# Fetching the norm factors of a hybrid decoder step as rows through DRAM instead of broadcasting them with matrix products

## The chip, the cores and the metric

The kernel runs on one core of a Trainium2 chip. The core has a matrix engine (TensorE, PE in the profile, with its weight loads as PEld), a vector engine (VectorE, DVE), a scalar engine (ScalarE, ACT), a general engine (GpSimd, POOL) and SyncE (SP), which here only issues DMA transfers, in order, and waits before each for what the transfer needs. ScalarE issues a few transfers as well. The metric is the device time of one launch in microseconds, as the median of several runs; lower is better.

## The reference

One layer of a hybrid decoder, run on 2048 prompt tokens and on 8 single tokens of a decode batch, all in fp32. What matters for this change are its five RMS norms:

```python
def _rmsnorm(x, g):
    xf = x.astype(jnp.float32)
    y = xf * lax.rsqrt(jnp.mean(xf * xf, axis=-1, keepdims=True) + EPS) * g.astype(jnp.float32)
    return y.astype(x.dtype)
...
    xn = _rmsnorm(x, norm1_g)
    z = jnp.einsum('btd,de->bte', xn, w_in)
    xr, gr, q, k, v = jnp.split(z, IN_SPLITS, axis=-1)
...
    rec = (hs * jax.nn.gelu(gr.astype(jnp.float32))).astype(x.dtype)
...
    mix = jnp.concatenate([_rmsnorm(rec, rec_norm_g), _rmsnorm(att, attn_norm_g)], axis=-1)
    h = x + jnp.einsum('bte,ed->btd', mix, w_out)
    hn = _rmsnorm(h, norm2_g)
    ff = jax.nn.silu(jnp.einsum('btd,df->btf', hn, w_gate)) * jnp.einsum('btd,df->btf', hn, w_up)
    y = h + jnp.einsum('btf,fd->btd', ff, w_down)
...
    y_prompt = _rmsnorm(yp, final_norm_g)
    y_sample = _rmsnorm(ys, final_norm_g)
```

`hs` is a gated linear recurrence over the tokens behind a short convolution, `att` a sliding-window attention with sinks. The model width is 1024, the two groups are 512 wide each, and the FFN is 2816 wide.

## The kernel before

**Layout and precision.** Activations lie transposed: features on the 128 partitions, tokens along the free dimension. A norm factor is one number per token, so it must be had on all 128 partitions as a row along the tokens before VectorE can multiply with it. The large products run in a fast fp32 mode on operands split into a high and a low part, three products for each pair; the small ones run in plain fp32, where the profile shows each as two instructions.

**First stage, the mixer.** The 2056 tokens are cut into four sub-blocks (`SUBS`: 520, 512, 512, 512 tokens). For each sub-block s the input projection runs as 14 units of 128 output columns (`unit`, L746, products named ip), in the order of `ORDERS[s]`: units 0 to 3 feed the recurrence, 4 to 7 the gate branch, 8 and 9 k and v, 10 to 13 q. A unit accumulates in one of three PSUM banks (pool `ps_acc`) and VectorE evacuates it with a multiplication by the row of factors of the first norm (L763). A gate unit is evacuated into `rrec`, of which there is one buffer for all sub-blocks, so the gate units of sub-block s wait until the group norm of sub-block s - 1 has scaled the old contents (the key `("rc", s - 1)`). Recurrence, attention, group norms (`group_norm`, L847), the output projection (`out_unit`, L1071; `out_half` for the last sub-block; products op) and the sum of squares for the second norm follow.

**Second stage, the FFN.** The tokens are cut again, into three blocks of two halves (`HALVES`: twice 344, then four times 342). `hn_mix` (L507) reads the residual stream `hs` back from DRAM, scales it with the factors of the second norm (L521), forms the sums and differences of a seven-product scheme (Strassen's) and stores them in DRAM as `mixed`; `hn_load` brings them back and splits them. For each block, 11 pairs of FFN chunks run gate, up (ps_g, ps_u) and down products (pd, pw), with y accumulated in SBUF by VectorE (L1469, L1500). `finish` (L1502) ends the first two blocks: it adds up squares, makes the final norm's factors, scales y (L1520) and stores it. `y_load` (L1214) then brings the residual stream of the next block into the same buffers. The third block ends in `finish_last`.

**How a factor row is made.** `rstd_cols` (L445) multiplies the accumulated squares with a column of averages on TensorE, which leaves one factor per partition in a few columns (104 x 5, 128 x 4, 86 x 4 or 114 x 3), adds epsilon on VectorE and raises to the power -0.5 on GpSimd (L454). For the first norm of sub-blocks 1 to 3 the squares come from ScalarE's accumulation instead (`norm_rows`, L656). Then `row_bcast` (L456) makes the row: for each column one plain fp32 product of the column, broadcast over 128 output rows, with the identity matrix, into the only bank of `ps_m`; ScalarE copies the result to SBUF (L470), into one of three buffers of `bcp`. `half_bcast` (L479) does the same for a half of a block of the second stage, from the factors `rs2` of all sub-blocks that it touches (copy at L494, two buffers of `hbp`).

**What sets the order of the work.** Every chain of work is a generator with planned times; the planned time becomes the priority with which a scheduler orders each engine's instructions. TensorE's order through the mixer and the start of the FFN is written out by hand in `PE_ORDER` (name and count of each product, from L112), with the broadcast products bc_x2, bc_x3, bc_rc1, bc_rc2 and the second norm's hb_0_0 and hb_0_1 in their places; later TensorE work is ordered by the scheduler. SP's transfers are ordered by the scheduler too, and a waiting transfer holds up all behind it.

Of the kernel before, what the change touches and what calls it, by code (L numbers as in the profile page):

```python
# [7 lines left out]
F32 = mybir.dt.float32  # L8
# [5 lines left out]
P = 128  # L14
# [4 lines left out]
NTOK = SEQ + NB  # L19
# [127 lines left out]
op0_6_260:2 s7_1_0:3 op0_6_260:10 op0_7_0:24 op0_7_260:3 o6_1_0 bc_x2_0:3 pt6_1_1 o6_1_0 bc_x2_0 op0_7_260 pt6_1_1:3  # L147
op0_7_260:11 o6_1_1 op0_7_260:9 ip2_4_0:24 o6_1_1 ip2_0_0:5 pt7_0_0:4 ip2_0_0:10 st_h0:5 ip2_0_0:2 o7_0_0 ip2_0_0:4
o7_0_0 ip2_0_0:3 ip2_5_0:4 pt7_0_1 st_rc1:2 pt7_0_1:3 st_rc1:2 ip2_5_0:9 pt7_1_0:4 ip2_5_0:2 o7_0_1 ip2_5_0:3 o7_0_1
bc_rc1_0:4 ip2_5_0:3 o7_1_0 ip2_5_0:3 pt7_1_1:3 ip2_1_0:2 pt7_1_1 ip2_1_0:8 g2_0_0_0 ip2_1_0:8 o7_1_0 ip2_1_0:4  # L150
# [7 lines left out]
op1_4_0:20 op1_5_0:3 pt9_0_1:4 op1_5_0 o9_0_0:2 op1_5_0:16 o9_0_1 op1_5_0:4 op1_6_0:2 bc_x3_0:2 s10_1_0 bc_x3_0:2  # L158
# [3 lines left out]
op1_7_0:8 s11_0_0 pt10_0_0:2 o9_1_1 s11_0_1 st_rc2:4 s11_0_1 op1_7_0:2 s11_0_1:2 op1_7_0:7 bc_rc2_0:4 op1_7_0:6  # L162
ip3_12_0 o10_0_0 ip3_12_0:3 o10_0_0 pt10_0_1:4 ip3_12_0:12 o10_0_1 ip3_12_0:3 s11_1_0:3 ip3_12_0:5 ip3_10_0:8
s11_1_1:4 pt10_1_0 st_h1:4 pt10_1_0:3 s11_1_0 ip3_10_0:4 o10_0_1 ip3_10_0:3 hb_0_0:4 ip3_10_0:6 o10_1_0 ip3_10_0:3
ip3_9_0 pt10_1_1 o10_1_0 pt10_1_1:3 ip3_9_0:8 hb_0_1:4 ip3_9_0:6 o10_1_1 ip3_9_0:9 ip3_11_0:2 o10_1_1 ip3_11_0
# [122 lines left out]
def hybrid_step(tc, xT, xR, vecs, cst, gatew, win, wout, wgate, wup, wdown, kT, vC, ck, cv, sconv, sh0,  # L288
# [4 lines left out]
    with ExitStack() as ctx:  # L293
# [54 lines left out]
        mixed = dp.tile([3, 7, P, 4, TP], F32, name="mixed")  # L348
        split_s = {x: dp.tile([NPAIR, 4, P, 2, 512], F32, name=f"split_{x}") for x in "gu"}
# [128 lines left out]

        def half_bcast(gi, n, name):  # L479
            o, nn = HALVES[gi][n]  # L480
            out = hbp.tile([P, TP], F32, tag="hb", name=f"hb_{name}")
            ps = m_tile(f"hb_{name}")
            for s, (c0, T, _, w, nt) in enumerate(SUBS):
                a, b = max(o, c0), min(o + nn, c0 + T)
                if a >= b:
                    continue
                j0, j1 = (a - c0) // w, (b - c0 - 1) // w + 1
                with ahead():
                    for j in range(j0, j1):
                        x, y = max(a, c0 + j * w), min(b, c0 + j * w + w)  # L490
                        d0 = x - c0 - j * w
# [93 lines left out]
        with ExitStack() as actx:  # L585
# [70 lines left out]
            def norm_rows(s, acc, sums):  # L656
                _, T, _, w, nt = SUBS[s]
                cols = ap1.tile([P, 5], F32, tag="xcols", name=f"xcols{s}")
                if s:
                    nc.vector.scalar_tensor_tensor(cols[:, :nt], sums[:, 0], EPS, sums[:, 1], ALU.add, ALU.add)  # L660
                    nc.gpsimd.tensor_tensor(cols[:, :nt], cols[:, :nt], nhalf[:, :nt], op=ALU.pow)
# [185 lines left out]
            def group_norm(s, raw, gcol, k0, name, t, keys, late=False):  # L847
                _, T, _, w, nt = SUBS[s]
                acc = None
                for c in range(CR):  # L850
                    yield (t - 8 + 2 * c,) + keys(c)
                    if c == 0:
                        acc = accp.tile([P, TM], F32, tag="acc", name=f"{name}acc{s}")
                    add_square(acc, raw[:, c, :T], T, c == 0, f"{name}{s}_{c}", nc.vector if s in V_GN else None)
                yield t
                cols = ap1.tile([P, 5], F32, tag=f"{name}cols", name=f"{name}cols{s}")
                rstd_cols(acc[:, :T], w, nt, 1, cols[:w, :nt], f"{name}{s}")
                bc = row_bcast(cols[:w, :nt], w, nt, f"{name}{s}")
                if late:
                    state[s]["late"] = bc  # L860
                    fire((name, s, "bc"))
                    return
                for c in range(CR):
                    yield t + 3 + c
                    v = raw[:, c, :T]
                    nc.vector.scalar_tensor_tensor(v, v, col(gcol + c), bc[:, :T], ALU.mult, ALU.mult)
# [204 lines left out]
            def out_unit(s, m):  # L1071
# [106 lines left out]
        with ExitStack() as bctx:  # L1178
# [323 lines left out]
            def finish(gi, n, t, dt):  # L1502
# [12 lines left out]
                yield t + dt * (F_FIN[2] + F_FIN[3])  # L1515
                bc = row_bcast(cols[:w, :nt], w, nt, name, 0, False, True)
# [65 lines left out]
            def last_norm(s):  # L1582
# [13 lines left out]
                rstd_cols(acc[:, :T], w, nt, 0, rs2[:w, s, :nt], f"h{s}", 0, True)  # L1596
                fire(("h", s))
# [132 lines left out]
```

## Time and profile before

| what | value |
|---|---|
| median of 3 runs | 2063.03 us (2059.93 to 2065.46) |
| span of the profiled execution | 2054.6 us |
| time of the profiled execution itself | not given; only its span is |
| TensorE busy | 2015.9 us, 98% |
| VectorE busy | 1459.9 us, 71% |
| ScalarE, GpSimd busy | 944.6 us (46%), 906.5 us (44%) |
| mean granted TensorE clock | 0.997 |
| DMA | 450.98 MB, mean 219 GB/s |

The span runs from the first to the last instruction of the profiled execution; the median, from other executions, is 8.4 us longer. All times inside the kernel count from the start of the span. Roughly, the mixer lasts until 690 us, with an overlap into the FFN, and the three FFN blocks end near 1150, 1610 and 2054 us. In a tile's row the numbers after the count are the shortest, median and longest duration in ns and the first and last start in us; in a row of the timeline or the chain they are start and duration in us. Matmuls are pipelined, so their durations overlap, and the chain shows what each adds. "Landing" is the time from the issue of a transfer until its data has arrived.

### The profile page before, as it was taken

How to read it: one execution, taken by the hardware profiler on the slowest of the kernel's cores; microseconds unless marked ns; L12 is line 12 of the kernel's file. 1: busy time of each engine (PE TensorE's matmuls, PEld its weight loads, DVE VectorE, ACT ScalarE, POOL GpSimd, SP SyncE). 2: the span in 40 equal slices, each digit the busy share in tenths (PEclk: the TensorE clock that was granted, in tenths of full speed). 3: DMA queues.
4: the chain of work that ended last, by engine and by line, in shares of the span. 5: the costliest groups of instructions: out<-in, count | busy, mean ns of one | idle time of the engine just before them, and what ended most of it. 6: DMA issues, size and time to landing. Idle time of an engine off the chain costs nothing.

```text
span 2054.6 us, 34857 instructions
## 1 busy us (share of the span) xinstructions
PE 2015.9 (98%) x12319; PEld 1908.1 (93%) x12319; DVE 1459.9 (71%) x2694; ACT 944.6 (46%) x1960; POOL 906.5 (44%) x799
## 2 busy tenths in 40 slices
PE   9999999999999999999999999999999999999998
PEld 9988787878777899999999999999999999999998
DVE  6877886767985766666654667777768666777675
ACT  6764774553664543343334533333335433433343
POOL 5311342020122787567656645556457522322333
PEclk9999999999999999999999999999999999999999
DMA  9864584576688856666546677776677675566652
GB/s 329 293 213 143 188 275 159 175 233 210 208 261 280 314 200 223 205 210 207 207 172 210 229 260 258 227 229 221 222 253 265 211 251 189 183 197 196 197 179 96
DMA packets 208991, 450.98 MB, mean 219 GB/s; under 512 B 25232, under 2 KB 82720, under 8 KB 208800
## 3 DMA queue, kind: packets, MB, share of 16 engines
q1 hardware_dynamic: 205184, 445.73, 65.2%
q10 hardware_dynamic: 3632, 3.02, 0.4%
q8 instruction: 97, 1.59, 0.3%
q14 instruction: 78, 0.64, 0.1%
HBM read 335.89 MB, written 113.84 MB: 219 GB/s over the span
## 4 chain that ended last, share of the span: by engine, by line
PE 77%; DVE 9%; DMA 6%; ACT 3%; issue 2%; POOL 1%; SPq 0%; DVEq 0%; ACTq 0%; POOLq 0%
PE ps_u L396 19%; PE ps_g L396 19%; PE pw L396 11%; PE pd L396 10%; PE ip L396 10%; PE op L396 4%; DMA n<-hs 3%; DMA xs<-in_xT 1%; DMA m<-mixed 1%; PE o L396 1%; PE pt L401 1%; DVE sc L974 1%; DVE sc L963 1%; PE s L396 1%; DMA mixed<-n 1%
## 5 line engine op out<-in xcount | busy, mean ns | idle before, releaser
L396 PE MATMUL ps_g<-hn,w_g 128*128 128x342 f32 (+1 forms) x2772 | 489.4, 320 | 4.6 <-DVE c_u L1410 1.8
L396 PE MATMUL ps_u<-hn,w_u 128*128 128x342 f32 (+1 forms) x2772 | 479.9, 319 | 1.9 <-ACT c_u L1436 1.3
L396 PEld LDWEIGHTS ps_g<-hn,w_g 128*128 128x128 f32 x2772 | 445.1, 188 | 6.0 <-DVE c_u L1410 2.3
L396 PEld LDWEIGHTS ps_u<-hn,w_u 128*128 128x128 f32 x2772 | 444.2, 188 | 2.6 <-ACT c_u L1436 1.6
L396 PE MATMUL ip<-xn,w_in 128*128 128x512 f32 (+1 forms) x1680 | 353.4, 358 | 1.9 <-ACT xn L431 1.8
L396 PEld LDWEIGHTS ip<-xn,w_in 128*128 128x128 f32 x1680 | 270.1, 189 | 46.0 <-issue 3.8
L1500 DVE TENSOR_TENSOR y<-y,pw 128x342 f32<-128x342 f32 x504 | 238.7, 504 | 73.0 <-PE pw L396 72.2
L396 PE MATMUL pd<-fh,w_d 128*128 128x344 f32 (+1 forms) x960 | 239.4, 320 | 0.6 <-DVE y L1469 0.6
L396 PE MATMUL op<-mix,w_out 128*128 128x512 f32 (+1 forms) x960 | 203.4, 357 | 0.5 <-DVE rrec L763 0.3
L396 PEld LDWEIGHTS op<-mix,w_out 128*128 128x128 f32 x960 | 155.4, 188 | 29.3 <-issue 5.0
L1469 DVE TENSOR_TENSOR y<-y,pd 128x344 f32<-128x344 f32 (+1 forms) x240 | 117.9, 507 | 75.3 <-PE pd L396 70.7
L396 PEld LDWEIGHTS pd<-fh,w_d 128*128 128x128 f32 x960 | 168.3, 188 | 1.4 <-DVE y L1469 1.1
L396 PE MATMUL pw<-fh,wd 128*128 128x342 f32 x576 | 165.6, 319 | 1.2 <-DVE y L1500 1.2
L396 PE MATMUL pd<-fl,w_d 128*128 128x344 f32 (+1 forms) x480 | 153.4, 320 | 0.0
L1381 DVE TENSOR_TENSOR fl<-c_u,fh 128x342 fp32r<-128x342 f32 (+1 forms) x132 | 107.1, 815 | 48.3 <-ACT fh L1380 47.9
L1225 POOL TENSOR_TENSOR w_u<-ru,w_u 128x512 fp32r<-128x512 f32 x44 | 58.9, 1338 | 181.6 <-ACT w_u L1224 155.0
L1392 POOL TENSOR_TENSOR c_u<-c_u,c_g 128x342 f32<-128x342 f32 (+1 forms) x60 | 60.5, 1008 | 170.7 <-DVE c_u L1410 132.1
L1380 ACT CAST fh<-c_u 128x342 fp32r<-128x342 f32 (+1 forms) x132 | 63.0, 480 | 157.8 <-POOL c_u L1392 61.9
L396 PE MATMUL pw<-t,wd 128*128 128x342 f32 x648 | 126.7, 320 | 2.6 <-DVE t L1381 1.7
L1410 DVE TENSOR_TENSOR c_u<-c_u,ps_u 128x342 f32<-128x342 f32 (+1 forms) x99 | 50.2, 507 | 100.3 <-PE ps_u L396 100.1
L396 PEld LDWEIGHTS pw<-t,wd 128*128 128x128 f32 x648 | 106.0, 188 | 4.4 <-DVE t L1381 2.5
L396 PEld LDWEIGHTS pw<-fh,wd 128*128 128x128 f32 x576 | 105.3, 189 | 1.7 <-DVE y L1500 1.5
(316 smaller groups left out, 3507.4 us busy)
## 6 DMA issues: line engine op xcount, KB each, us to landing
w_g<-split_g SPq DMA_DIRECT2D x88, 512.0 KB, 4.2
w_u<-split_u SPq DMA_DIRECT2D x88, 512.0 KB, 4.9
w_in<-split_w SPq DMA_DIRECT2D x84, 512.0 KB, 3.5
rg<-in_wgate SPq DMA_DIRECT2D x110, 256.0 KB, 3.1
ru<-in_wup SPq DMA_DIRECT2D x110, 256.0 KB, 3.2
w_out<-split_w SPq DMA_DIRECT2D x48, 512.0 KB, 4.4
split_g<-w_g SPq DMA_DIRECT2D x44, 512.0 KB, 3.6
split_u<-w_u SPq DMA_DIRECT2D x44, 512.0 KB, 2.7
```

What stands on the lines that cost most here:

```text
L396: r = nc.tensor.matmul(*args, **kw)
L401: r = nc.tensor.transpose(*args)
L963: seen[f"sm{gb}_{kv}_{g}"] = nc.vector.tensor_tensor_reduce(sc[:, g, :kn], ps[:, gi * 256:gi * 256 + kn], mask[:, k0:k0 + kn], -SCALE, ns[ ...
L974: nc.vector.tensor_scalar(sc[:, g, :kn], sc[:, g, :kn], mx[:, 1, g:g + 1], None, ALU.mult)
L1225: lo_eng.tensor_tensor(w[:, 1, :], src, w[:, 0, :].bitcast(F32), op=ALU.subtract)
L1380: nc.scalar.copy(hi, v)
L1381: nc.vector.tensor_tensor(lo, v, hi.bitcast(F32), ALU.subtract)
L1392: (nc.vector if p == NPAIR - 1 or src is not v else eng(E_MUL[2 * h + n])).tensor_tensor(v, src, g, op=ALU.mult)
L1410: nc.vector.tensor_tensor(o, a, b, op)
L1469: r = nc.vector.tensor_tensor(ys[gi, n, m], ys[gi, n, m], ps, ALU.add)
L1500: nc.vector.tensor_tensor(v, v, ps, ALU.add)
```

## The change

Some rows of factors no longer come from broadcast products. Their columns are stored to DRAM as a row of single words, and a second transfer reads the row back onto all 128 partitions. Both transfers are issued by SP. This holds for the first norm of sub-blocks 2 and 3 (x2, x3), the recurrent group's norm of sub-blocks 1 and 2 (rc1, rc2), all six half rows of the second norm, and the final norm of the first two blocks. The second norm's factors are stored once for each of the four sub-blocks, as soon as they are made. The other rows keep the broadcast products. In `finish` the planned delay ahead of the row goes as well.

```diff
+        rows_h = dp.tile([1, NTOK], F32, name="rows_h")
...
+        def rows_out(row, cols, w, nt):
+            nc.sync.dma_start(row.rearrange("o (j p) -> p (o j)", p=w), cols)
+
+        def dram_bcast(cols, w, nt, name):
+            row = dp.tile([1, w * nt], F32, name=f"row_{name}")
+            rows_out(row, cols, w, nt)
+            out = bcp.tile([P, TM], F32, tag="bc", name=f"rb_{name}")
+            nc.sync.dma_start(out[:, :w * nt], row.to_broadcast([P, w * nt]))
+            return out
+
+        def h_rows(s):
+            c0, T, _, w, nt = SUBS[s]
+            rows_out(rows_h[:, c0:c0 + T], rs2[:w, s, :nt], w, nt)
+
         def half_bcast(gi, n, name):
             o, nn = HALVES[gi][n]
             out = hbp.tile([P, TP], F32, tag="hb", name=f"hb_{name}")
-            ps = m_tile(f"hb_{name}")
-            for s, (c0, T, _, w, nt) in enumerate(SUBS):
...
-                        mm(f"hb_{name}", ps[:, x - o:y - o], rs2[:w, s, j:j + 1].to_broadcast([w, P]),
-                                         ident[:w, d0:d0 + y - x], start=True, stop=True)
-            nc.scalar.copy(out[:, :nn], ps[:, :nn])
+            nc.sync.dma_start(out[:, :nn], rows_h[:, o:o + nn].to_broadcast([P, nn]))
             return out
...
-                state[s]["bc"] = row_bcast(cols[:w, :nt], w, nt, f"x{s}")
+                state[s]["bc"] = (dram_bcast if s > 1 else row_bcast)(cols[:w, :nt], w, nt, f"x{s}")
...
-                bc = row_bcast(cols[:w, :nt], w, nt, f"{name}{s}")
+                bc = (dram_bcast if name == "rc" and s in (1, 2) else row_bcast)(cols[:w, :nt], w, nt, f"{name}{s}")
...
                     rstd_cols(acc[:, :T], w, nt, 0, rs2[:w, s, :nt], f"h{s}")
+                    h_rows(s)
                     fire(("h", s))
...
                 rstd_cols(acc[:, :nn], w, nt, 0, cols[:w, :nt], name, 0, True)
-                yield t + dt * (F_FIN[2] + F_FIN[3])
-                bc = row_bcast(cols[:w, :nt], w, nt, name, 0, False, True)
+                bc = dram_bcast(cols[:w, :nt], w, nt, name)
...
                 rstd_cols(acc[:, :T], w, nt, 0, rs2[:w, s, :nt], f"h{s}", 0, True)
+                h_rows(s)
                 fire(("h", s))
```

In `PE_ORDER` the entries bc_x2_0, bc_x3_0, bc_rc1_0, bc_rc2_0, hb_0_0 and hb_0_1 are taken out; the rest of the order stands.

More of the change, by code (lines that the diff above doesn't have):

```diff
@@ L157 @@
 pt8_1_1:4 op1_3_0:18 op1_4_0 g2_3_1_0 op1_4_0:3 o8_1_1 s10_0_0:4 o8_1_1 s10_0_1 pt9_0_0:2 s10_0_1:3 pt9_0_0:2
-op1_4_0:20 op1_5_0:3 pt9_0_1:4 op1_5_0 o9_0_0:2 op1_5_0:16 o9_0_1 op1_5_0:4 op1_6_0:2 bc_x3_0:2 s10_1_0 bc_x3_0:2
+op1_4_0:20 op1_5_0:3 pt9_0_1:4 op1_5_0 o9_0_0:2 op1_5_0:16 o9_0_1 op1_5_0:4 op1_6_0:2 s10_1_0
 s10_1_0:3 op1_6_0:2 o9_0_1 op1_6_0 s10_1_1:4 op1_6_0 pt9_1_0:2 op1_6_0:3 pt9_1_0:2 op1_6_0:5 ip3_8_0 op1_6_0 ip3_8_0
@@ L161 @@
 op1_6_0 o9_1_0 op1_6_0 ip3_8_0 pt9_1_1 o9_1_0 ip3_8_0:5 pt9_1_1:3 ip3_8_0:9 op1_7_0 o9_1_1 s11_0_0:3 pt10_0_0:2
-op1_7_0:8 s11_0_0 pt10_0_0:2 o9_1_1 s11_0_1 st_rc2:4 s11_0_1 op1_7_0:2 s11_0_1:2 op1_7_0:7 bc_rc2_0:4 op1_7_0:6
+op1_7_0:8 s11_0_0 pt10_0_0:2 o9_1_1 s11_0_1 st_rc2:4 s11_0_1 op1_7_0:2 s11_0_1:2 op1_7_0:7 op1_7_0:6
 ip3_12_0 o10_0_0 ip3_12_0:3 o10_0_0 pt10_0_1:4 ip3_12_0:12 o10_0_1 ip3_12_0:3 s11_1_0:3 ip3_12_0:5 ip3_10_0:8
-s11_1_1:4 pt10_1_0 st_h1:4 pt10_1_0:3 s11_1_0 ip3_10_0:4 o10_0_1 ip3_10_0:3 hb_0_0:4 ip3_10_0:6 o10_1_0 ip3_10_0:3
-ip3_9_0 pt10_1_1 o10_1_0 pt10_1_1:3 ip3_9_0:8 hb_0_1:4 ip3_9_0:6 o10_1_1 ip3_9_0:9 ip3_11_0:2 o10_1_1 ip3_11_0
+s11_1_1:4 pt10_1_0 st_h1:4 pt10_1_0:3 s11_1_0 ip3_10_0:4 o10_0_1 ip3_10_0:3 ip3_10_0:6 o10_1_0 ip3_10_0:3
+ip3_9_0 pt10_1_1 o10_1_0 pt10_1_1:3 ip3_9_0:8 ip3_9_0:6 o10_1_1 ip3_9_0:9 ip3_11_0:2 o10_1_1 ip3_11_0
 pt11_0_0:4 ip3_11_0:16 vt3_0 ip3_11_0:5 ip3_13_0:3 pt11_0_1 o11_0_0:2 ip3_13_0 pt11_0_1:3 ip3_13_0:4 vt3_1
@@ L481, in half_bcast @@
             out = hbp.tile([P, TP], F32, tag="hb", name=f"hb_{name}")
-            ps = m_tile(f"hb_{name}")
-            for s, (c0, T, _, w, nt) in enumerate(SUBS):
[L484 to L491, printed above, removed]
-                        mm(f"hb_{name}", ps[:, x - o:y - o], rs2[:w, s, j:j + 1].to_broadcast([w, P]),
-                                         ident[:w, d0:d0 + y - x], start=True, stop=True)
-            nc.scalar.copy(out[:, :nn], ps[:, :nn])
+            nc.sync.dma_start(out[:, :nn], rows_h[:, o:o + nn].to_broadcast([P, nn]))
             return out
```

4 lines of the change are left out of this document (2 added, 2 removed).

## The prediction

> **What bounds the kernel now.** I read the page first, engines and chain.
>
> ```profile
> PE 2015.9 (98%) x12319; PEld 1908.1 (93%) x12319; DVE 1459.9 (71%) x2694; ACT 944.6 (46%) x1960; POOL 906.5 (44%) x799
> PE 77%; DVE 9%; DMA 6%; ACT 3%; issue 2%; POOL 1%; SPq 0%; DVEq 0%; ACTq 0%; POOLq 0%
> ```
>
> TensorE is busy for 98% of the span, and 77% of the chain that ended last is TensorE's own work. Busy alone proves little, since matmul ends are modelled, but the chain agrees: an instruction taken out of TensorE's stream is worth its pitch wherever TensorE is what ends last. The stages (columns: PE, PEld, DVE, ACT, POOL, clock, DMA share, GB/s) show where it isn't.
>
> ```profile
> 600.00:650.00 50.00, 47.13 (x233) 37.66 (x232) 37.94 (x78) 28.52 (x60) 16.45 (x14) 1.00 0.83 269
> 650.00:700.00 50.00, 45.65 (x244) 39.78 (x243) 36.89 (x50) 21.45 (x44) 27.84 (x20) 1.00 0.96 344
> ```
>
> At the passage from the mixer to the FFN the DMA engines are at 0.83 to 0.96 and TensorE stands idle for 2.87 + 4.35 = 7.2 us. A matmul removed there only lengthens the idle time.
>
> **What goes.** The tiles that the change takes from TensorE, the first two in windows that hold sub-blocks 2, 3 and 1, 2 alone, the last in one that holds the first two block ends alone:
>
> ```profile
> L396 PE MATMUL bc_x<-cs,xcols x16: 270/275/275, 294.5 to 438.8; 128*128 128x128 f32 x16
> L396 PE MATMUL bc_rc<-cs,rccols x16: 270/275/275, 318.4 to 459.8; 128*128 128x128 f32 x16
> L396 PE MATMUL hb<-cs,rs x44: 166/275/356, 473.9 to 1158.1; 128*128 128x128 f32 x16, 104*128 104x104 f32 x8, 104*128 104x32 f32 x2, 104*128 104x72 f32 x2
> L396 PE MATMUL bc_f<-cs,cols_f x28: 239/275/275, 1183.7 to 1639.3; 86*128 86x86 f32 x16, 114*128 114x114 f32 x12
> ```
>
> That is 16 + 16 + 44 + 28 = 104 instructions (each fp32 product shows as two). Their 275 ns overlap, so I take what they add to the chain:
>
> ```profile
> 459.19 0.89 PE bc_rc L396 x8
> 474.11 0.81 PE hb L396 x8
> 480.08 0.82 PE hb L396 x8
> ...
> 1153.11 0.82 PE hb L396 x8
> 1157.70 0.67 PE hb L396 x6
> ...
> 1183.85 0.86 PE bc_f L396 x8
> 1188.38 0.86 PE bc_f L396 x8
> ...
> 1634.56 0.66 PE bc_f L396 x6
> 1638.87 0.66 PE bc_f L396 x6
> ```
>
> Four rows of x2, x3, rc1, rc2 at 0.89 each are 3.56; block 0's two half rows 1.63; block 2's 1.49; the block ends 1.72 and 1.32. Block 1's 14 instructions lie off the chain; at 0.82/8 they are 1.44. Together 11.16 us. The 14 ScalarE copies go as well; ScalarE is 46% busy and I give them nothing.
>
> **What comes.** Each factor row now takes two transfers in sequence on SP: a store of 344 to 520 single words, which waits for POOL's power and scatters column by column, and a load that puts the row on 128 partitions, which waits for the store to land. (The second norm has four stores for six loads.) The trace has neither. Nearest:
>
> ```profile
> n<-hs SPq DMA_DIRECT2D x32, 171.0 KB, 3.7
> xs<-in_xT SPq DMA_DIRECT2D x24, 256.0 KB, 4.6
> out_sh_o<-q ACTq DMA_DIRECT2D x4, 4.0 KB, 2.1
> out_sconv_o<-in_sconv SPq DMA_DIRECT2D x1, 32.0 KB, 8.6
> out_phs<-carry ACTq DMA_DIRECT2D x1, 2.0 KB, 5.2
> ```
>
> The load has the size and partitions of n or xs: 3.7 to 4.6 us. The store, of 1.3 to 2 KB, lies between 2.1 (4 KB of short runs on a quiet queue) and 8.6 (short runs behind two large copies); out_phs, the nearest in size, took 5.2 at a moment of full queues. I take 3.0, nearer the quiet end, as most stores fall outside the crowded passage. With two issue gaps of about 0.2 the trip is 3.0 + 4.2 + 0.4 = 7.6 us after the power; bounds 2.1 + 3.7 + 0.4 = 6.2 and 8.6 + 4.6 + 0.4 = 13.6. Where the products stood late in TensorE's order a row can also arrive sooner than before (the second norm, below).
>
> The Trainium skill, page "DMA: Bandwidth & Descriptors", section "Anatomy of one DMA — SWDGE (gpsimd) path", gives each transfer a fixed 2.0 us and 436 GB/s: 4.6 us for the pair, an estimate. No row here is as short, and by it the sum below would be 0.8 better, since rc1 would not stall.
>
> Now user by user.
>
> *x2, x3:* hidden. The powers end long before the row is used:
>
> ```profile
> 123.76 1.02 POOL L661 TENSOR_TENSOR xcols<-xcols,nhalf 128x4 f32<-128x4 f32 x1 [7.86 <-DVE xcols L660]
> ...
> 426.13 1.02 POOL L661 TENSOR_TENSOR xcols<-xcols,nhalf 128x4 f32<-128x4 f32 x1 [5.09 <-DVE xcols L660]
> 442.79 0.57 ACT L470 COPY rb_x<-bc_x 128x512 f32<-128x512 f32 x1
> ```
>
> x3's power is done at 427.15 and the row stood ready at 443.36. Even 13.6 us leaves 2.6; without that cover the first evacuation of sub-block 3 would slip by what is missing. The load for x2 has to wait for a free row buffer (three exist), but its product stood at 294.5 and its power ends at 124.78.
>
> *rc2:* hidden. Its users are the mix tiles of the output projection of sub-block 2 and gate unit 4 of sub-block 3, eighth in ORDERS[3], seven units after the row. Unhidden it would cost what rc1 can.
>
> *rc1:* tight. Gate unit 4 is first in ORDERS[2]; its product can't be evacuated into rrec until rc1 has scaled the old contents, and it holds one of three accumulator banks until then.
>
> ```profile
> 314.71 1.01 POOL L454 TENSOR_TENSOR rccols<-rccols,nhalf 128x4 f32<-128x4 f32 x1
> 320.10 2.74 DVE L866 SCALAR_TENSOR_TENSOR rrec<-rrec,vec,rb_rc 128x512 f32<-128x512 f32 x4 [0.21 <-ACT rb_rc L470]
> 325.16 0.68 DVE L763 TENSOR_TENSOR rrec<-ip,rb_x 128x512 f32<-128x512 f32 x1
> 328.99 10.31 PE L396 MATMUL ip<-xn,w_in 128*128 128x512 f32 x42
> ```
>
> Power to scaling takes 320.10 - 315.72 = 4.4 us; the bank is free at 325.84, and the written order has 24 products of unit 8 and 18 of unit 12 (the 42) start at 328.99: 3.15 us of slack, less the 0.89 that TensorE now gains between them, 2.3. The trip adds 7.6 - 4.4 = 3.2 (bounds 1.8 and 9.2): a stall of 0.9, from nothing to 6.9. VectorE runs four scalings and three subtractions before that evacuation and may close part of it, so I charge 0.8. Behind a waiting scaling on VectorE stand the evacuations of the attention (L985, L997), for which TensorE's transposes and value products wait.
>
> *Second norm:* block 0's half rows.
>
> ```profile
> 472.02 1.02 POOL L454 TENSOR_TENSOR rs<-rs,nhalf 128x4 f32<-128x4 f32 x1 [5.47 <-DVE rs L453]
> 482.08 1.06 DVE L521 SCALAR_TENSOR_TENSOR n<-n,vec,hb 128x344 f32<-128x344 f32 x2
> ```
>
> The first mix begins 9.0 us after the power, because the hand-written order put the second half row late. The trip of 7.6 fits, with one more load. Blocks 1 and 2 find their rows in DRAM well ahead; block 1's two loads (342 KB) fall into the passage at 344 GB/s: +1.0. Their saving of 1.44 falls there too and isn't counted.
>
> *Block ends:* the power, then the scaling of y, its store, the load of the next y, the adds that free TensorE's banks.
>
> ```profile
> 1182.46 1.01 POOL L454 TENSOR_TENSOR cols_f<-cols_f,nhalf 86x4 f32<-86x4 f32 x1
> 1191.87 3.98 DVE L1520 SCALAR_TENSOR_TENSOR y<-y,vec,rb_f 128x344 f32<-128x344 f32 x8
> 1203.19 0.93 DVE L1469 TENSOR_TENSOR y<-y,pd 128x342 f32<-128x342 f32 x2 [1.90 <-DMA y<-hs]
> 1632.04 0.86 POOL L454 TENSOR_TENSOR cols_f<-cols_f,nhalf 114x3 f32<-114x3 f32 x1
> 1641.07 3.97 DVE L1520 SCALAR_TENSOR_TENSOR y<-y,vec,rb_f 128x342 f32<-128x342 f32 x8
> ```
>
> From the later power to its scaling there are 1191.87 - 1183.47 = 8.4 us at the first end and 8.2 at the second. The trip of 7.6 fits by under a microsecond. At the first end the adds already wait for y, so TensorE, 1.72 earlier, meets the same y: I count half of that saving away, 0.86.
>
> *SP's queue:* each store holds SP until its power, each load until its store has landed.
>
> ```profile
> SPq L380 <- PE ip L396: 160.1, 62, 5.2
> ```
>
> Weight loads stand behind. SP itself already waits for free buffers, 160.1/62 = 2.6 us each time and up to 5.2, and five weight buffers of 12 products cover such a wait; I charge nothing, and if the cover is gone each held load costs TensorE the excess over it.
>
> **Sum:** -11.16 + 1.44 + 0.86 + 0.8 + 1.0 = -7.1 us. The profiled span of 2054.6 becomes 2047.5. The median of the runs, 2063.03, stands 8.4 above the span (no time of the profiled run itself is given), so 2063.03 - 7.1 = 2055.9; I say 2056.
>
> **Rivals.** (a) *The saving is taken up elsewhere.* Of the 11.16, 5.2 us lie before the passage (3.56 + 1.63). If the passage is fixed by VectorE and DMA work that doesn't move with TensorE, they turn into idle time there; what is left, 1.49 + 1.32 + 0.86 - 1.0 = 2.7, gives about 2060. For it speaks the idle time of 7.2; against it that the chain before 500 us is TensorE's, so that VectorE's inputs come earlier as well.
>
> (b) *Slower: the block ends become the bound.* One mechanism: the store of a last row comes late, the scaling after it, the next y after that, and the adds leave TensorE without banks. It decides once the trip exceeds 8.4 us. With a store of 5.2, a load of 4.6, 0.4 of gaps and one SP wait of 5.2 in front it is 15.4: 7.0 and 7.2 late, 14.2 in both. An idle TensorE is also slowed afterwards:
>
> ```profile
> 204.00:212.00 8.00, 5.29 (x23) 3.19 (x23) 7.48 (x16) 6.38 (x15) 0.00 (x0) 0.93 0.00 0
> 212.00:220.00 8.00, 8.00 (x43) 7.10 (x43) 7.60 (x12) 4.18 (x8) 3.29 (x2) 0.86 0.01 2
> ```
>
> After 2.7 us of idleness the granted clock fell, which costs 8 x 0.07 + 8 x 0.14 = 1.7; twice 3.4. In all -7.1 + 14.2 + 3.4 = +10.5: 2073.5; with the upper bound of the trip behind the same wait (18.8, 21.0 late in both) 2080, and down to 2069 where one end alone is hit hard. For it speaks that by the code SP issues 16 stores and 16 loads of y there; against it that the median landings are short.
>
> The Trainium skill, same page, section "Why a DMA increments its semaphore by 16 and not by 1", says a transfer spreads over the largest number up to 16 that divides its outer size: a store of 86 columns would use 2 engines and of 114 columns 6. No row here shows such a shape; by that rule (b) would be likelier at the first end than at the second.
>
> (c) *More than the sum.* The first mix can start 9.0 - 7.6 = 1.4 to 9.0 - 6.2 = 2.8 us sooner, and its chain of loads and stores with it, so that VectorE is freer before the passage. With no charge at all (11.16 - 1.44 = 9.7) that makes 11.1 to 12.5, 2050.5 to 2052. Against it, most of that chain waits for its own loads.
>
> (d) *The store or load isn't made as said, and the products stay:* the diff removes them from the written order, which pops each by name, so this has no chance worth a share.
>
> **How the numbers follow.** About 0.3%, 6.2 us, is what a measurement of this kernel can tell from no change: faster means below 2056.8. Forecast 0.55, from 2052 to 2060; its middle lies just past the bound, and since each of the charges (0.8, 0.86, 1.0) can be nought I put 0.36 of it to faster and 0.19 to same. (a) 0.19, same. (b) 0.17, slower. (c) 0.09, faster. Faster 0.45, same 0.38, slower 0.17. The range from 2050 to 2070 leaves out most of (b), 0.15, and little else; it is the forecast's own range with (c) below and the mild end of (b) above. The forecast alone, 2052 to 2060, would hold with (a) 0.74.
>
> **What would show it.** TensorE with 104 instructions fewer; new rows on SP with landings of 2 to 5 us for the stores and about 4 for the loads; VectorE's scaling by rc1 about 8 us after the power and TensorE's unit 8 starting within a microsecond of bank release; no gap at TensorE near the two block ends. Wrong: gaps there of several microseconds, a clock below 1.00 in those stages, or idle time in the passage grown by 5 us (rival a).

## The result, and the profile after

| kernel | median | range |
|---|---|---|
| before | 2061.48 us | 2058.70 to 2065.46 (4 runs) |
| changed | 2138.47 us | 2136.63 to 2141.61 (4 runs) |

The ratio is 1.0376 (95% interval 1.0362 to 1.0391): 77 us slower, where 7 us faster was forecast. The profiled span grew from 2054.6 to 2139.8 us. (The changed kernel's lines after the new functions are numbered one to four higher.) First the page of the changed kernel, engines and chain:

```profile
PE 2030.2 (95%) x12215; PEld 1912.0 (89%) x12215; DVE 1456.5 (68%) x2694; ACT 938.3 (44%) x1946; POOL 907.2 (42%) x799
PE 61%; DMA 15%; DVE 12%; issue 4%; ACT 4%; POOL 3%; SPq 1%; DVEq 0%; POOLq 0%; ACTq 0%
```

The 104 instructions are gone (12319 to 12215), yet TensorE is busy for 14.3 us longer, and its idle time (span less busy) went from 38.7 to 109.6 us, by 70.9: together the 85.2 of the span. The chain that ended last gives DMA 15% in place of 6%.

The transfers that the change added, from the list of DMA issues (count, size, median us from issue to landing):

```profile
rows_h<-rs SPq DMA_DIRECT2D x3, 2.0 KB, 9.5
row_x<-xcols SPq DMA_DIRECT2D x2, 2.0 KB, 9.7
rb_x<-row_x SPq DMA_DIRECT2D x2, 256.0 KB, 5.5
rb_f<-row_f SPq DMA_DIRECT2D x2, 171.0 KB, 4.2
```

The loads of 171 to 256 KB take 4.2 to 5.5 us, where about 4 was forecast. The stores of 2 KB take twice as long as the loads, where 3.0 was forecast. A row's trip is seen in the timeline; here rc1, first POOL, then SP, then VectorE, then TensorE:

```profile
315.91 1.01 POOL L455 TENSOR_TENSOR rccols<-rccols,nhalf 128x4 f32<-128x4 f32 x1
```

```profile
312.41 0.33 SPq L481 DMA_DIRECT2D rows_h<-rs  x1
...
319.24 0.32 SPq L497 DMA_DIRECT2D hb<-rows_h  x1
319.66 0.38 SPq L481 DMA_DIRECT2D row_rc<-rccols  x1
...
331.11 0.32 SPq L487 DMA_DIRECT2D rb_rc<-row_rc  x1
```

```profile
320.39 0.68 DVE L1000 TENSOR_TENSOR ratt<-o,ratt 64x512 f32<-64x512 f32 x1 [0.86 <-ACT ratt L999]
336.75 2.74 DVE L869 SCALAR_TENSOR_TENSOR rrec<-rrec,vec,rb_rc 128x512 f32<-128x512 f32 x4 [15.68 <-DMA rb_rc<-row_rc]
```

```profile
339.48 0.79 PE L397 MATMUL o<-pth,vt 128*128 128x512 f32 x1 [10.54 <-ACT pth L987]
```

The power ends at 316.92. SP is then still in front of a load of the second norm that waits for its own store (312.41 to 319.24, 6.8 us), and issues rc1's store only at 319.66. The load, which waits for that store to land, goes out at 331.11: 11.4 us. It lands at 336.7. From the power to the scaling it takes 19.8 us, against 4.4 before. VectorE, which works in order, stands in front of that scaling for 15.68 us; the attention's evacuations queue behind it, and TensorE stops for 10.54 us. The mean clock granted is lower in such a stop and after it (the number ahead of the DMA share and GB/s):

```profile
328.00:336.00 8.00, 0.94 (x5) 0.42 (x3) 0.00 (x0) 0.00 (x0) 0.00 (x0) 0.83 0.53 41
336.00:344.00 8.00, 4.30 (x8) 2.37 (x9) 7.25 (x12) 5.73 (x10) 0.00 (x0) 0.53 0.51 192
```

Over the whole execution the mean granted clock is 0.981, against 0.997 before. That is enough to make TensorE busy for longer with less work: an estimate from 2015.9 us less the 11.16 saved, times 0.997/0.981, is 2037 us, and 2030.2 was measured. VectorE waits in the same way for both rows of rc, for all four rows of the block ends and once for the second norm, but not for x2 and x3 (total us, times, longest):

```profile
DVE y L1523 <- DMA rb_f<-row_f: 33.7, 4, 10.5
DVE rrec L869 <- DMA rb_rc<-row_rc: 28.7, 2, 15.7
DVE n L524 <- DMA hb<-rows_h: 7.4, 1, 7.4
```

These are 69.8 us; before, VectorE waited 3.2 us in all for the copies of such rows. At the first block end SP and VectorE read:

```profile
1231.51 0.25 SPq L481 DMA_DIRECT2D row_f<-cols_f  x1
...
1239.59 0.32 SPq L487 DMA_DIRECT2D rb_f<-row_f  x1
...
1241.96 0.26 SPq L481 DMA_DIRECT2D row_f<-cols_f  x1
...
1249.48 0.32 SPq L487 DMA_DIRECT2D rb_f<-row_f  x1
```

```profile
1243.58 4.46 DVE L1523 SCALAR_TENSOR_TENSOR y<-y,vec,rb_f 128x344 f32<-128x344 f32 x8 [10.46 <-DMA rb_f<-row_f]
...
1253.89 3.01 DVE L1523 SCALAR_TENSOR_TENSOR y<-y,vec,rb_f 128x344 f32<-128x344 f32 x6 [5.43 <-DMA rb_f<-row_f]
```

Stores of 8.1 and 7.5 us, and the second held on SP behind the first row's load until 1241.96. TensorE's two waits there are for VectorE's adds:

```profile
1248.51 0.65 PE L397 MATMUL pd<-fh,w_d 128*128 128x342 f32 x1 [4.97 <-DVE y L1473]
...
1257.38 3.79 PE L397 MATMUL ps_g<-hn,w_g 128*128 128x342 f32 x12 [4.61 <-DVE c_g L1414]
```

At the second end the two stores take 6.6 and 10.9 us, and TensorE waits 3.20 and 8.97.

### The profile page after: what moved, and what is told of

Its sections match the earlier page's. It is cut to its first block, busy times and chain, and to the rows that moved or that the text cites. A ratio compares the mean times of both kernels' runs of the same rounds, so it can differ in the third digit from the quotient of the medians.

```text
span 2139.8 us, 34674 instructions
## 1 busy us (share of the span) xinstructions
PE 2030.2 (95%) x12215; PEld 1912.0 (89%) x12215; DVE 1456.5 (68%) x2694; ACT 938.3 (44%) x1946; POOL 907.2 (42%) x799
## 4 chain that ended last, share of the span: by engine, by line
PE 61%; DMA 15%; DVE 12%; issue 4%; ACT 4%; POOL 3%; SPq 1%; DVEq 0%; POOLq 0%; ACTq 0%
PE ps_u L397 17%; PE ps_g L397 16%; PE pw L397 9%; PE pd L397 9%; PE ip L397 6%; DMA n<-hs 3%; DMA row_f<-cols_f 2%; PE op L397 1%; DMA hs<-xres 1%; DMA row_rc<-rccols 1%; DMA m<-mixed 1%; DMA mixed<-n 1%; DVE sc L977 1%; DMA rows_h<-rs 1%; DVE xn L433 1%
## 5 line engine op out<-in xcount | busy, mean ns | idle before, releaser
L397 PE MATMUL ps_g<-hn,w_g 128*128 128x342 f32 (+1 forms) x2772 | 494.2, 322 | 20.1 <-DVE c_g L1414 13.6
L397 PE MATMUL ip<-xn,w_in 128*128 128x512 f32 (+1 forms) x1680 | 358.1, 361 | 2.4 <-ACT xn L432 1.7
L397 PEld LDWEIGHTS ip<-xn,w_in 128*128 128x128 f32 x1680 | 274.4, 192 | 48.1 <-issue 4.1
L397 PE MATMUL pd<-fh,w_d 128*128 128x344 f32 (+1 forms) x960 | 241.6, 323 | 14.2 <-DVE y L1473 14.2
L1385 DVE TENSOR_TENSOR fl<-c_u,fh 128x342 fp32r<-128x342 f32 (+1 forms) x132 | 109.6, 836 | 49.1 <-ACT fh L1384 48.9
```

Of the source, the lines that this page charges most:

```text
L397: r = nc.tensor.matmul(*args, **kw)
L1385: nc.vector.tensor_tensor(lo, v, hi.bitcast(F32), ALU.subtract)
```

## The experiments

The theory after this result: the store of single words is the slow thing, and it also holds the other transfers. Rivals: any trip through DRAM is this slow, or SP's order is the cost. Each ratio is to the kernel before, run beside it, with the 95% interval.

| label | what | median us | ratio |
|---|---|---|---|
| e1_runs16 | as changed, stores as 16-byte runs | 2071.91 | 1.0055 (1.0034 to 1.0076) |
| e2_dead_stores | before, plus the word stores, unread | 2095.71 | 1.0171 (1.0145 to 1.0198) |
| e7_dead_runs16 | the same as 16-byte runs | 2059.43 | 1.0003 (0.9992 to 1.0014) |
| e11_dead_apart16 | e2, words 16 bytes apart | 2058.58 | 1.0000 (0.9987 to 1.0013) |
| e10_dead_apart64 | e2, words 64 bytes apart | 2059.07 | 0.9995 (0.9985 to 1.0005) |
| e8_dead_apart | e2, words 512 bytes apart | 2058.27 | 1.0001 (0.9990 to 1.0012) |
| e4_x_h_only | as changed, x2, x3, second norm only | 2083.40 | 1.0115 (1.0097 to 1.0134) |
| e3_act_queue | as changed, rows issued by ScalarE | 2127.27 | 1.0330 (1.0309 to 1.0350) |
| e12_rc2_later | as changed, rc2 scaling planned later | 2123.96 | 1.0314 (1.0292 to 1.0335) |
| e13_same | the changed kernel again | 2128.06 | 1.0327 (1.0311 to 1.0342) |
| e14_rc2_held | as changed, rc2 scaling moved | 2119.93 | 1.0289 (1.0274 to 1.0305) |
| e15_act_again | e3 again, beside e13 | 2127.69 | 1.0317 (1.0299 to 1.0335) |
| e5_turned | as changed, rows turned first | 2064.82 | 1.0032 (1.0020 to 1.0045) |
| e9_turned_no_ends | e5 without the block ends | 2061.65 | 1.0016 (1.0005 to 1.0027) |
| e6_turned_slack | e5 at x2, x3, second norm only | 2056.11 | 0.9986 (0.9977 to 0.9995) |

**Larger pieces.** e1_runs16:

```diff
-            nc.sync.dma_start(row.rearrange("o (j p) -> p (o j)", p=w), cols)
+            nc.sync.dma_start(row.rearrange("o (p j) -> p (o j)", p=w), cols)
```

> The changed kernel with one line altered: the factors' columns go to the row in DRAM partition by partition, so that each partition writes 4 or 5 neighbouring words (16 or 20 bytes) in place of 4 or 5 words that lie 344 to 512 bytes apart. 128 writes in place of 512; the loads, the queue and every wait stay as they are. The row's words then lie in another order, so the factors meet other tokens and the values are not the reference's. Theory (the store of single words is what is slow, 7 to 12 us each, and it holds the other transfers): the store falls to 2 to 4 us, the trips of rc1 and rc2 from 17 to 20 us to 8 to 11, and most of the 77 us comes back: 2055 to 2085 us. Rival one (any store and load through DRAM takes this long, whatever its pieces): trips and time stay, 2128 to 2145 us. Rival two (SP's order is the cost: transfers queued behind a load that waits for its store): the waits get shorter only by what the store does, so with stores still above 6 us 2115 to 2140 us.

Most of the 77 us came back; 12 stayed. The issues of e1, and VectorE's waits:

```profile
rows_h<-rs SPq DMA_DIRECT2D x3, 2.0 KB, 2.1
row_x<-xcols SPq DMA_DIRECT2D x2, 2.0 KB, 3.1
```

```profile
DVE y L1523 <- DMA rb_f<-row_f: 12.0, 3, 5.2
DVE rrec L869 <- DMA rb_rc<-row_rc: 5.1, 2, 4.4
DVE n L524 <- DMA hb<-rows_h: 2.2, 1, 2.2
```

The same bytes, places, queue and waits, with stores of 2.1 and 3.1 us in place of 9.5 and 9.7. The rival "any trip is that slow" falls, and SP's order alone with it.

**Stores that nobody reads.** e2_dead_stores keeps every product of before and adds the stores:

```diff
+                if s > 1:
+                    rows_out(dp.tile([1, w * nt], F32, name=f"row_x{s}"), cols[:w, :nt], w, nt)
                 state[s]["bc"] = row_bcast(cols[:w, :nt], w, nt, f"x{s}")
```

and so at the other sites.

> The kernel before, with its broadcast products kept and used, and beside them the same stores of the factors into DRAM rows that the changed kernel makes (x2, x3, rc1, rc2, the four of the second norm, the four of the final norm), which nobody reads. No instruction waits for a store to land. Theory (the store of single words also holds the other transfers of the queues for some microseconds, and 512 writes at twelve places are enough to be felt): 5 to 25 us slower than before, 2066 to 2086 us, with waits of TensorE for weight or residual loads behind the stores. Rival (only the chain power, store, load, scaling costs; a store by itself is free): 2056 to 2067 us, within 0.3% of before. If it comes above 2100 us, the holding of the queues, not the trip, would be most of the cost.

35 us slower, above the theory's 5 to 25: the stores cost nearly half of the loss with no reader at all. How they do it is seen on SP in the passage to the FFN, and on TensorE:

```profile
643.27 0.39 SPq L481 DMA_DIRECT2D rows_h<-rs  x1
...
647.04 0.32 SPq L381 DMA_DIRECT2D w_out<-split_w  x1
654.55 0.32 SPq L591 DMA_DIRECT2D m<-mixed  x1
```

```profile
655.17 2.07 PE L397 MATMUL op<-mix,w_out 128*128 128x512 f32 x4 [4.14 <-DVE xres L1149]
...
1229.81 1.48 PE L397 MATMUL ps_u<-hn,w_u 128*128 128x342 f32 x4 [6.85 <-DMA w_u<-split_u]
```

After the store SP gets out four more transfers and then stands until 654.55, because an earlier load of `mixed` lands late (SP waits 6.1 us for it); the residual's load goes out behind it, and TensorE waits. At 1229.81 it waits for its weights themselves. The packets' own records say the same: in the kernel before no packet of up to 8 KB took over 3 us (longest 2.6); in the changed kernel 73 did (longest 10.1), in e2 61. They also show when the time goes, here for rc1's store in the changed kernel, issued at 319.66: 544 of the 576 four-byte packets up to its landing pass between 322.7 and 323.5 us. Then the core's DMA moves next to nothing (6 GB/s, the last number) while packets of 4 KB of a weight load stand for up to 6.2 us, and the last 16 four-byte packets follow only from 327.3 on:

```profile
324.50:331.00 6.50, 4.44 (x18) 2.96 (x16) 0.00 (x0) 0.00 (x0) 0.00 (x0) 1.00 0.25 6
```

By these records the words themselves are passed on quickly; the delay comes behind them, and for other transfers too.

**What it is about the words.** The same dead stores as runs (16 or 20 bytes, 12 at the second block end), then single words at three distances. The edit of the runs is that of e1; that of the spaced words, against e2:

```diff
-            nc.sync.dma_start(row.rearrange("o (j p) -> p (o j)", p=w), cols)
+            nc.sync.dma_start(row[:, :1].rearrange("(j p) o -> p (o j)", p=w), cols)
...
-        rows_h = dp.tile([1, NTOK], F32, name="rows_h")
+        rows_h = dp.tile([NTOK, 128], F32, name="rows_h")
```

(128 for e8, 16 for e10, 4 for e11; the other rows likewise.)

> The kernel before with the stores that nobody reads, as 128 writes of 16 or 20 bytes in place of 512 of 4 bytes (the same bytes, places, queue and waits). Theory (the single words are what holds the other transfers): the 35 us of the dead word stores go, 2056 to 2070 us. Rival (a store put into SyncE's order costs by its wait and its issue, not by its pieces): 2080 to 2100 us.

> The kernel before with the dead word stores, each word 512 bytes from the next in DRAM in place of 4 bytes (the row's neighbours then share no line). If the slowness is that neighbouring words of one line are written by different DMA engines and wait for each other, it goes: stores of 2 to 4 us, 2056 to 2070 us. If it is the number of writes below some size (512, each about 15 ns one after the other), it stays: stores of 7 to 12 us, 2085 to 2105 us.

> The kernel before with the dead word stores, each word 64 bytes from the next (512 bytes apart cost nothing, neighbours 37 us). If a line of 64 bytes or less is what two words must not share: as with 512 bytes apart, 2054 to 2064 us. If it is a block larger than 64 bytes: 2064 to 2100 us.

> The kernel before with the dead word stores, each word 16 bytes from the next. The number of writes stays 512 for a row; a line of 64 bytes gets 4 of them in place of 16, as it does from the runs of 16 bytes (which cost nothing with 128 writes). If the cost goes by writes that share a line, a part of the 37 us stays: 2060 to 2085 us. If it needs a line of 32 bytes or less: between that and none, 2054 to 2070 us. If it goes by sharing at all: 2085 to 2105 us.

None of the four can be told from the kernel before. Their three stores of the second norm, first e2's neighbours, then e11, e10, e8 and e7:

```profile
rows_h<-rs SPq DMA_DIRECT2D x3, 2.0 KB, 8.1
```

```profile
rows_h<-rs SPq DMA_DIRECT2D x3, 2.0 KB, 3.2
```

```profile
rows_h<-rs SPq DMA_DIRECT2D x3, 2.0 KB, 2.8
```

```profile
rows_h<-rs SPq DMA_DIRECT2D x3, 2.0 KB, 2.4
```

```profile
rows_h<-rs SPq DMA_DIRECT2D x3, 2.0 KB, 2.9
```

The other transfers go on as well. In the 8 us behind one of these stores, in the passage to the FFN, e2's core moves 46 GB/s and e11's 207 (e2 first):

```profile
643.60:651.60 8.00, 7.43 (x35) 5.68 (x33) 1.66 (x3) 0.77 (x2) 0.00 (x0) 1.00 0.74 46
```

```profile
638.00:646.00 8.00, 8.00 (x38) 6.47 (x37) 3.84 (x7) 2.24 (x5) 0.00 (x0) 1.00 0.73 207
```

e2, e11, e10 and e8 make the same number of 4-byte writes. So neither the size of a write nor their number is enough; the words must also lie closer than 16 bytes to each other, each written by itself. No packet of up to 8 KB took over 3 us in any of these four. e11's expectation, that four writes in a line of 64 bytes would still cost, fell. In these stores such neighbours always come from different partitions; whether that is needed isn't shown, since neighbouring words written singly by one partition weren't tried. What goes on in the memory isn't seen in the trace. e2 ran on another chip than e7 and e8, and these on another than e10 and e11; that the chips make the difference isn't excluded, but neighbouring words were slow on all three chips on which they are known to have run, and e1's runs were quick on e2's chip.

**A part of the change.** e4_x_h_only leaves rc1, rc2 and the block ends with their products:

```diff
-                bc = (dram_bcast if name == "rc" and s in (1, 2) else row_bcast)(cols[:w, :nt], w, nt, f"{name}{s}")
+                bc = (dram_bcast if name == "rc" and s in () else row_bcast)(cols[:w, :nt], w, nt, f"{name}{s}")
```

(`s in ()` is never true. The products of rc1 and rc2 go back into `PE_ORDER`, and the block ends get their `row_bcast` again.)

> A part of the change alone: rows through DRAM for x2, x3 and the second norm; rc1, rc2 and the block ends by broadcast products as before. Theory by the staircase of TensorE's delay in the changed kernel (x3 about 3, second norm about 2 + 6 + 8, less the some 5 us that the left out products save, nothing from rc and the ends): 8 to 20 us slower than before, 2069 to 2082 us. Rival one (the delay moves: time that rc1 and rc2 take hides what x3 and the second norm would take, which appears when those are gone): over 2085 us. Rival two (the cost lies in rc and the ends alone): 2052 to 2066 us.

23 to 24 us, just over the theory's range and under the first rival's. Aligned with the kernel before, TensorE's delay grows by 8.4 near x3's use, where 3 was expected, and by 6.0 to 6.7 at each of three stores of the second norm. VectorE waits 7.95 us there for a store of the residual (1.71 before); whether that one was held by words or came late in SP's order stays open.

**Who waits.** In e3_act_queue ScalarE issues the new stores and loads (`nc.scalar.dma_start` for `nc.sync.dma_start` in the four new calls).

> The changed kernel with all its new stores and loads of rows issued by ScalarE instead of SyncE, so that no weight or residual load on SyncE stands behind a load that waits for its store; ScalarE now stands at that wait, and its own copies behind it. Theory (the slow store and VectorE's order are the cost): the trips keep their stores of 7 to 12 us and lose only the 3 to 10 us for which SyncE was held (rc1, the second half at the block ends), but ScalarE's copies of the psum tiles wait in their place: 2110 to 2160 us. Rival (SyncE's order is most of the cost): at least 30 us come back, 2065 to 2108 us.

It came out 11 us under the changed kernel, but the two were run at different times. e12_rc2_later tried VectorE's order by a planned time:

```diff
-                    yield t + 3 + c
+                    yield t + 3 + c + (14 if name == "rc" and s == 2 else 0)
```

> The changed kernel with one number altered: the scaling by rc2 and its mix tiles get a planned time 14 us later, so that they stand later in VectorE's order; store, load, queue and TensorE's written order stay. The first user of the scaled tiles comes some 50 us after the power. Theory (a slow row costs because VectorE, which works in order, stands in front of its scaling and everything behind it waits): VectorE's wait of 13.0 us and TensorE's of 12.8 us there go, and with them 10 to 18 us: 2118 to 2129 us. Rival (the word store holds the transfers, and TensorE would wait for its weights or residuals there anyway): 2131 to 2142 us, with a wait for a DMA in place of the one for VectorE.

Inconclusive: the edit left the scaling where it was in VectorE's order (VectorE still waited 11.0 us in front of it), and yet the time was 14 us lower, spread over the whole span. So the changed kernel itself was run again, beside two others.

> The changed kernel, unaltered, beside the next two on the same chip, to see how far its own time moves. If its time is steady: 2134 to 2143 us. If the time that the word stores take differs from chip to chip, as 2124 us with an almost unaltered order suggests: 2115 to 2134 us, with VectorE's waits for the rows shorter in proportion.

2128.06 us, 10 us less than the first time, while the kernel before stood at 2060.17 (2061.48 the first time): the cost of the word stores is not the same each time. The runs were on several chips, so whether the chip or the time makes it isn't shown. VectorE's waits for rows add up to 62.4 in place of 69.8. Set beside the first measurement, e3 and e12 prove nothing; e15 and e14, beside e13, can be read.

> Stores and loads of rows issued by ScalarE once more, beside the unaltered changed kernel on the same chip. If SyncE's order costs the some 10 us that the first run showed: 5 to 15 us under the unaltered one. If that difference was between chips: within 5 us of it.

The same time as e13. VectorE's wait for rc fell, and ScalarE's came in its place; e15's VectorE row, then its largest ScalarE rows of this kind:

```profile
DVE rrec L869 <- DMA rb_rc<-row_rc: 5.1, 2, 2.6
```

```profile
ACT c_g L1440 <- DMA row_f<-cols_f: 13.9, 2, 8.7
...
ACT sq_h L443 <- DMA row_rc<-rccols: 12.4, 1, 12.4
ACT pth L987 <- DMA rows_h<-rs: 10.8, 1, 10.8
```

Freeing SP is worth nothing here if ScalarE has to stand instead. e14_rc2_held moves the one scaling by a dependency:

```diff
+                gain = col
+                if name == "rc" and s == 2:
+                    yield t + 3, ("q", 3, 0)
+                    held = ap1.tile([P, CR], F32, tag="heldg", name="heldg")
+                    for c in range(CR):
+                        nc.vector.scalar_tensor_tensor(held[:, c:c + 1], qraw[:, 0, :1], 0.0, col(gcol + c), ALU.mult, ALU.add)
+                    gain = lambda i: held[:, i - gcol:i - gcol + 1]
...
-                    nc.vector.scalar_tensor_tensor(v, v, col(gcol + c), bc[:, :T], ALU.mult, ALU.mult)
+                    nc.vector.scalar_tensor_tensor(v, v, gain(gcol + c), bc[:, :T], ALU.mult, ALU.mult)
```

> The changed kernel with the scaling by rc2 moved in VectorE's order by a real dependency: its gain column is made by four tiny instructions that also read a query tile of sub-block 3 (times nought), so that the scaling stands behind that tile's evacuation. Store, load, SyncE's order and TensorE's written order stay. Theory (VectorE's order): VectorE's wait for the row of rc2, 13.0 us in the changed kernel, falls below 3, TensorE's wait of 12.8 us there goes, and the time lies 8 to 16 us under that of the unaltered changed kernel in the same call. Rival (the held transfers would stop TensorE there anyway): within 5 us of it.

8.1 us less than e13, at the near end of the theory's range. First e13's VectorE, then e14's:

```profile
490.67 2.74 DVE L869 SCALAR_TENSOR_TENSOR rrec<-rrec,vec,rb_rc 128x512 f32<-128x512 f32 x4 [11.31 <-DMA rb_rc<-row_rc]
...
512.29 1.06 DVE L524 SCALAR_TENSOR_TENSOR n<-n,vec,hb 128x344 f32<-128x344 f32 x2 [6.52 <-DMA hb<-rows_h]
```

```profile
505.91 1.06 DVE L524 SCALAR_TENSOR_TENSOR n<-n,vec,hb 128x344 f32<-128x344 f32 x2 [12.75 <-DMA hb<-rows_h]
...
509.81 2.74 DVE L876 SCALAR_TENSOR_TENSOR rrec<-rrec,heldg,rb_rc 128x512 f32<-128x512 f32 x4
```

No wait is left in front of rc2's scaling (11.31 us in e13). TensorE gains 12.9 us there against e13 and gives 8.9 back at once: VectorE now stands in front of the next late row, the second norm's, for 12.75 us in place of 6.52. So about 4 of the 8.1 us are seen at rc2; where the others come from isn't shown. At rc2 VectorE's order is thus shown as the way from a late row to an idle TensorE, and also that one late row had covered for the next.

**Turned rows.** In e5_turned TensorE first turns the columns, so that 3 to 5 partitions each store one long run:

```diff
-        def rows_out(row, cols, w, nt):
-            nc.sync.dma_start(row.rearrange("o (j p) -> p (o j)", p=w), cols)
+        def rows_out(row, cols, w, nt, stage):
+            ps = m_tile("rt")
+            with ahead():
+                tr("rt", ps[:nt, :w], cols, ident[:w, :w])
+            nc.scalar.copy(stage[:nt, :w], ps[:nt, :w])
+            nc.sync.dma_start(row.rearrange("o (j p) -> j (o p)", p=w), stage[:nt, :w])
```

The staging place is the buffer that the row will be loaded into, or the spent accumulator. e9 leaves the block ends to products, e6 also rc1 and rc2.

> The changed kernel with the factors' columns turned first: one TensorE product against the identity makes of the 86 to 128 partitions x 4 or 5 columns 4 or 5 partitions x 86 to 128 words, ScalarE copies that out of psum, and the store then writes 4 or 5 runs of 344 to 512 bytes. All sites go through DRAM as in the changed kernel; the values are the reference's. Theory (512 or so writes of single words are what is slow): the store lands in about 2 us, the trip gets about 1 us of product and copy, and the time is near that of the kernel with 16-byte runs (2072 us): 2058 to 2080 us. Rival (it is the partition count or the target, not the size of the pieces, and few long runs gain nothing over 16-byte ones but pay for product and copy): 2078 to 2095 us.

> As the turned kernel, but only where the prediction saw slack: x2, x3 and the second norm go through DRAM as turned runs; rc1, rc2 and the block ends keep their broadcast products. Theory (what is left in the kernel with 16-byte runs is the longer trip at rc1 and the block ends, 4 us each in its staircase, while x2, x3 and the second norm have the time): 2050 to 2063 us, at or a little under the kernel before. Rival (the second norm's loads and stores on SyncE cost as well, whatever the store's shape): 2064 to 2080 us.

> The turned kernel without the block ends: x2, x3, rc1, rc2 and the second norm through DRAM as turned runs, the final norm by broadcast products as before. It stands between the kernel with all sites (2064.8 us) and the one with the slack sites (2056.1 us), 8.7 us apart. Theory by the staircases: the ends give 4 to 6 us each there, of which the products that come back take 3, so 2057 to 2061 us. Rival (the 5 us steps at rc1 and rc2 are what stays, and the ends' steps are time that was due anyway): 2062 to 2067 us.

e5 is 0.3% slower than before, and VectorE still waits:

```profile
DVE y L1527 <- DMA rb_f<-row_f: 15.1, 4, 5.0
DVE rrec L873 <- DMA rb_rc<-row_rc: 8.0, 2, 4.7
```

e6, without those, waits for one row, 0.9 us in all, and is 0.14% faster than the kernel before (0.05 to 0.23%), some 3 us: the only version here that is clearly faster, by less than the 0.3% named in the prediction. From e6 to e9 the ratio rises by 0.0030 (6 us, rc1 and rc2) and on to e5 by 0.0016 (3 us, the block ends). e9 came out at the line between its two expectations; more of the rest lies in rc than the theory said.

## Why the prediction was wrong

*The saving.* The 104 instructions went. Their 11.16 us were never seen whole, since each way of getting the rows through DRAM put waits in their place; where there were next to none (e6), the outcome of some 3 us (1 to 5 by its interval) fits the pitches of x2, x3 and the second norm (1.78 + 1.63 + 1.49 = 4.9) less six added products.

*The store: the step that failed.* "I take 3.0, nearer the quiet end": it took 6.6 to 11.7 us. The rows chosen as nearest were alike in bytes, but none of them wrote neighbouring words singly; by the experiments that likeness was the one that counted. The load, taken as 4.2, took 4.2 to 5.5. The trip came to 19.8 us at rc1, beyond the upper bound of 13.6: 11.4 for the store and 5.6 for the load pass it already, and 2.7 came on top, in which another row's load held SP.

*The store's cost to others* had no term. e2 prices it at 35 us with no reader, e7 at nothing with 16-byte runs.

*rc2 "hidden"*: this failed for another reason. The users of the scaled tiles do come late, but the scaling itself stands where it stood in VectorE's order, and VectorE waits there, and TensorE for VectorE:

```profile
497.73 2.74 DVE L869 SCALAR_TENSOR_TENSOR rrec<-rrec,vec,rb_rc 128x512 f32<-128x512 f32 x4 [13.04 <-DMA rb_rc<-row_rc]
```

```profile
507.20 0.80 PE L397 MATMUL o<-pth,vt 128*128 128x512 f32 x1 [12.77 <-DVE ratt L1000]
```

The prediction named what is queued behind rc1's scaling, and then counted rc2's slack from the last user. e14 shows that step.

*rc1*: the place was right; the bounds (0 to 6.9) were passed (10.5 us of idle TensorE), and the stall came by the attention's evacuations, which the prediction named without a charge, not by gate unit 4's bank. With stores of 2 to 4 us (e1) VectorE waits 4.4 us there.

*Second norm*: "The trip of 7.6 fits": VectorE waited 7.4 us for the first row. With turned rows (e6) it waits 0.9.

*The block ends*: rival (b), given 0.17, had the mechanism and the threshold (a trip over 8.4 us); trips were 10.9 to 21.4 us. It priced 14.2 + 3.4 us for both ends; TensorE's delay grew by about 11 to 14 at each. Its path, the next y's loads, was not what TensorE waited for: VectorE's adds stood directly behind the waiting scaling.

*SP's queue at nothing*: SP does stand, for 11 us at rc1. But e15 doesn't get that back by moving it to ScalarE.

*With the store as forecast* (e1) the time is 2072 us, still 2 beyond the range: rc1's scaling then began 8.6 us after its store was issued (316.35 to 324.90), and VectorE waited up to 5.2 us at the block ends, where the trip was to fit "by under a microsecond".

If the parts simply add, which isn't shown: the trips with short stores cost about 12 + 11 = 23 us (e1's loss, and the saving that should have shown); the words add some 56 to 66 us to that, of which 35 need no reader. The remaining 21 to 31 would be what the readers' waits add; that part is only a difference, and e14 shows about 4 of it at rc2.

The Trainium skill, page "DMA: Bandwidth & Descriptors", section "Specifications", gives 512 B as the least transfer for line rate and says that below it the DMA engine reads, modifies and writes back. By that rule alone e8, e10 and e11, with 4-byte writes, should cost what e2 does; at 2.4 to 3.2 us a store against 8.1 they don't, so it does not by itself explain the slow stores. The rule of the Trainium skill that the prediction cited (same page, section "Why a DMA increments its semaphore by 16 and not by 1"), on how many engines a shape gets, would have made the first block end (86 partitions, which the prediction calls columns) the worse one; the stores took 8.1 and 7.5 us there and 6.6 and 10.9 at the second, and TensorE's waits were 4.97 + 4.61 us and 3.20 + 8.97, so no run here bears it out. The 4.6 us for a store and a load, which the prediction worked out from the Trainium skill, rest on a section of that page about transfers issued by GpSimd; these are issued by SP, and with short stores (e1) rc1's trip took 8.6 us.

## What to carry to other kernels

Before a transfer is priced by a row of the same size, look at which words lie side by side in its target and who writes them: a column per partition stored as single words that are neighbours in DRAM is to be turned first, or stored in runs (12 to 20 bytes were enough here). And slack is not counted from the last user of a value but from the place of its first instruction in the order of its engine; an engine that works in order hands the wait on to everything behind it. A stall that goes may only uncover the next one, so a single removal can be worth less than its wait.

## What the runs showed of the hardware

- 342 to 520 single words written next to each other from 86 to 128 partitions landed in 6.6 to 11.7 us; by the medians shown, such words 16, 64 or 512 bytes apart landed in 3.2, 2.8 and 2.4, and as 16-byte runs in 2.1 to 3.1 us.
- Such a store slows the other transfers on the queues: packets of up to 8 KB, which take at most 2.6 us in the kernel before, took up to 10.1. Behind rc1's store, whose four-byte packets had nearly all passed in 0.8 us, the core's DMA moved 6 GB/s for 6.5 us.
- The cost of these stores changed by an eighth from one time and chip to another (77 and 68 us for the same kernel), when the kernel without them changed by 0.1%.
